# The last half of the final norm, in two pieces of 160 tokens, with two of eight tiles on GpSimd

## The chip, the core and the metric

The kernel runs on one core of a Trainium2 chip. The metric is device time in microseconds (us): the median of several runs, 925.3 us for the kernel before (three runs, 924.67 to 925.98). Beside the timed runs there is one profiled execution, from which every view below is taken; times inside it are counted from the start of its span.

## The reference, cut to what matters

The program computes one layer of a hybrid attention backbone for 128 prompt tokens and 512 latent tokens (640 in all, 1024 features), with an MLP of 4096 hidden features, and then a final RMS norm. Only the end concerns us:

```
x = x + gate2 * SquaredReLU-MLP(RMSNorm(x) * (1 + scale2) + shift2)
y = x * rsqrt(mean(x * x) + 1e-6) * final_norm_g
```

The mean runs over the 1024 features of one token.

## The kernel before

Activations lie with features on the partitions: 1024 features are eight tiles `X1[0]` to `X1[7]` of 128 partitions, each with 640 token columns in two halves of 320 (`HALVES`, also `L0` and `L1`). Float32 accuracy is had by splitting operands in a high and a low part, so that each product is three matmuls (L1657 to L1659).

The MLP is four chunks `c` of hidden features, each done as seven block products per pair of output tiles (`A11`, `A12`, `S3`, `A22`, `S2`, `S1`, `S4`) in the order of the list `SEQ`. A product is 12 matmuls into one PSUM bank. `layer2` then folds the bank into the residual: `gate_half` multiplies by the gate and adds to `X1` (VectorE, L1510). In the last chunk each finished half tile goes to `done_half`: ScalarE squares it (L1525), VectorE adds the squares up (L1529), ScalarE multiplies the tile by the norm's gain (L1530). For the second half of the tokens the tiles are finished in the order 1, 3, 5, 7 (`S1`), 0, 2, 4, 6 (`S4`); the last two squares are not added but summed by a matmul of their own (`NSUM[1] = 2`, list `direct[1]`). So the very last product of the program is `S4` with `n = 3`, and it finishes tile 6 of the second half.

With the last tile of a half, `done_half` appends nine small steps to the list `side`. The first, `norm`, sums acc and direct squares over the partitions with a matrix of ones (float32 matmuls, L1537) into a bank, and makes the reciprocal root from it as Exp(-0.5 Ln(mean + eps)) on ScalarE (L1541, L1542), kept in the SBUF tile `rstd3`. The other eight, `final(0)` to `final(7)`, multiply one half tile by the root on VectorE (L1546) and store it (L1547): even tiles on the SP queue, odd tiles on ScalarE's queue, 160 KB each. The main loop takes one step of `side` after each product (L1684), and all that are left when the products are through (L1686). The first half's steps lie in the same list, five empty steps behind its last product (`LAG3`); in the program text its last six `final` steps stand behind the last `gate_half`.

That text is not the order on the engines. The order written by hand ends at L1616; after it the framework places each instruction by when it expects its inputs, and it may put a later one ahead of an earlier one that is not ready. It also sets all waits between engines.

Of the kernel before, what the change touches and what calls it, by code (L numbers as in the profile page):

```python
# [12 lines left out]
AF = mybir.ActivationFunctionType  # L13
OP = mybir.AluOpType
# [4 lines left out]
HT = 320  # L19
KT = 8  # L20
# [42 lines left out]
NSUM = (1, 2)  # L63
# [2 lines left out]
P3 = 8  # L66
GPV = 1
LOACC = (("in", 21, 22), ("in", 29, 30), ("in", 20, 24), ("in", 25, 26), ("in", 28, 34), ("br", 0, 8))
FINP = ()
HALVES = (slice(0, HT), slice(HT, NT))  # L70


# [1 line left out]
def trunk_layer(ctx: ExitStack, tc: tile.TileContext, xT, small_in, wmodA, wmodB, tabs, cacheK, cacheV, bias,  # L74
                w_in, w_br, w_out, w1, w2, yT, akT, avT, bkT, bvT):
    nc = tc.nc
    PE, ACT, DVE = nc.tensor, nc.scalar, nc.vector
# [29 lines left out]
    def u(name, dt=F32):  # L107
        return cur["p"].tile([P, NT], dt, tag="u", bufs=cur["nu"], name=name)
# [10 lines left out]
    def tt_tile(name):  # L119
        return cur["p"].tile([P, NT], F32R, tag="tt", bufs=12, name=name)  # L120
# [22 lines left out]
    def r32(ap):  # L143
        return ap.bitcast(F32)
# [11 lines left out]
    gn = pk[:, 322:346].rearrange("p (k n) -> p k n", k=3)  # L156
    ones = cst.tile([P, P], F32, name="ones")
    DVE.memset(ones, 1.0 / 1024.0)
    eps = cst.tile([P, 1], F32, name="eps")
# [38 lines left out]
    def sq_add(acc, x, f, sl):  # L198

        q = acc if f == 0 else u("sq")  # L200
        ACT.activation(q[:, sl], x[:, sl], AF.Square)
        if 0 < f < KT - 1:
            DVE.tensor_add(acc[:, sl], acc[:, sl], q[:, sl])
        return q
# [933 lines left out]
    class Units:  # L1138
        n = 0
# [17 lines left out]
    for n in range(KT):  # L1157
# [4 lines left out]
        for i, w in enumerate((wa, wb)):  # L1162
            for h in range(2):
                if w is None:
                    s = u("sg")
# [68 lines left out]
    X1 = {}  # L1234
# [3 lines left out]
    for n, h in order(KT, 4):  # L1238
# [8 lines left out]
        sq = sq_add(acc2, X1[n], n, HALVES[h])  # L1247
# [31 lines left out]
    L0, L1 = slice(0, HT), slice(HT, NT)  # L1279
# [143 lines left out]
    def bank():  # L1423
        return pp8[0].tile([P, 512], F32, tag="b", bufs=8, name="b")[:, :HT]
# [22 lines left out]
    def opd(c, name):  # L1447
        if (c, name) not in OPD:
            OPD[c, name] = (bp[0].tile([P, 8, HT], F32R, tag="op3", bufs=1, name="op") if len(OPD) % 3 == 2 else
                            m.tile([P, 8, HT], F32R, tag="op", bufs=2, name="op"))  # L1450
        return OPD[c, name]
# [53 lines left out]
    def gate_half(i, src, h, g=None):  # L1505
        g = (mods if g is None else g)[:, 24 + i]

        off = HALVES[h].start
        for sl, j in SEGS[h]:
            DVE.scalar_tensor_tensor(X1[i][:, sl], src[:, sl.start - off:sl.stop - off], g[:, j:j + 1],  # L1510
                                     X1[i][:, sl], op0=OP.mult, op1=OP.add)

    nrm = {0: [], 1: []}
    direct = {0: [], 1: []}

    def done_half(i, h):

        x, first_, last_ = X1[i][:, HALVES[h]], not nrm[h], len(nrm[h]) == KT - 1
        if first_:
            nrm[h].append(tt_tile("acc3"))  # L1520
        else:
            nrm[h].append(None)
        acc = r32(nrm[h][0][:, L0])
        q = acc if first_ else r32(tt_tile("sq3")[:, L0])
        ACT.activation(q, x, AF.Square)  # L1525
        if len(nrm[h]) > KT - NSUM[h]:
            direct[h].append(q)
        elif not first_:
            (nc.gpsimd if SQP else DVE).tensor_add(acc, acc, q)  # L1529
        ACT.activation(x, x, AF.Copy, scale=gn[:, 2, i:i + 1])  # L1530
        if last_:
            rs = r32(tt_tile("rstd3")[:, L0])

            def norm():
                b = bank()
                for k, a in enumerate([acc] + direct[h]):
                    PE.matmul(b, ones, a, start=k == 0, stop=k == NSUM[h])  # L1537
                if POW:
                    DVE.tensor_scalar(rs, b, EPS, -0.5, op0=OP.add, op1=OP.pow)
                else:  # L1540
                    ACT.activation(rs, b, AF.Ln, bias=eps)  # L1541
                    ACT.activation(rs, rs, AF.Exp, scale=-0.5)  # L1542

            def final(f):
                y = X1[f][:, HALVES[h]]
                (DVE if h or f not in FINP else nc.gpsimd).tensor_mul(y, y, rs)  # L1546
                (nc.sync, nc.scalar)[f % 2].dma_start(yT[:, f, HALVES[h]], y)  # L1547
            side.extend([lambda: None] * (0 if h else LAG3) + [norm] + [lambda f=f: final(f) for f in range(KT)])

    WS = [None] * 4  # L1550

# [5 lines left out]
    def layer2(c, n, o, b, p):  # L1557
        if c < 3:
            if o == "A11":
                WS[n] = tp1.get()  # L1560
                ACT.activation(WS[n], b, AF.Copy)  # L1561
                gate_half(2 * n, WS[n] if GPV else b, 1)
            elif o == "S3":
                DVE.tensor_add(WS[n], WS[n], b)
            else:
                e, h = {"A12": (0, 0), "A22": (1, 0), "S2": (1, 0), "S1": (1, 1), "S4": (0, 1)}[o]
                gate_half(2 * n + e, b, h, neg if o == "S4" else None)
            return
        if o == "A11":
            p.pv = tp1.get()  # L1570
            ACT.activation(p.pv, b, AF.Copy)
            gate_half(2 * n, b, 1)
        if o == "A12":
            gate_half(2 * n, b, 0)
            done_half(2 * n, 0)
        if o == "S3":
            DVE.tensor_add(p.pv, p.pv, b)
        if o == "A22":
            p.x = tp2.get()
            DVE.tensor_sub(p.x, b, p.pv)  # L1580
            gate_half(2 * n + 1, p.pv, 1, neg)
        if o == "S2":
            DVE.tensor_add(p.x, p.x, b)
            gate_half(2 * n + 1, p.x, 0)
            done_half(2 * n + 1, 0)
        if o == "S1":
            gate_half(2 * n + 1, b, 1)
            done_half(2 * n + 1, 1)
        if o == "S4":
            gate_half(2 * n, b, 1, neg)  # L1590
            done_half(2 * n, 1)

# [5 lines left out]
    neg = parts[:, 1]  # L1598
# [15 lines left out]
    for n, h in todo:  # L1614
# [7 lines left out]
        e, i = n % 2, n // 2  # L1622
# [20 lines left out]
    for x in SEQ:  # L1643
        l, c, n, o = x
# [3 lines left out]
        else:  # L1648
            s = opd(c, XOF[o])
# [3 lines left out]
        b = getattr(p, "b" + whole) if whole else bank()  # L1653
        setattr(p, "b" + o, b)
        for k in range(4):
            xh, xl = xk(k)
            PE.matmul(b, w[:, k], xh, start=not whole and k == 0, stop=False, skip_group_check=True)  # L1657
            PE.matmul(b, w[:, k], xl, start=False, stop=False, skip_group_check=True)  # L1658
            PE.matmul(b, w[:, 4 + k], xh, start=False, stop=o not in ("A11", "S2", "S1") and k == 3, skip_group_check=True)  # L1659
        (layer1 if l == 1 else layer2)(c, n, o, b, p)  # L1660
        W.live -= 1
        if l == 1 and o in ("A12", "S2") and n > 1:
# [127 lines left out]
```

## Time and profile before

| quantity | value |
| --- | --- |
| median of three runs | 925.3 us |
| time of the profiled execution | 923.14 us |
| its span, first to last instruction | 921.4 us |
| granted TensorE clock, mean | 0.997 |
| TensorE matmul busy | 903.8 us, 98% |
| VectorE busy | 712.9 us, 77% |
| ScalarE busy | 564.4 us, 61% |
| GpSimd busy | 194.6 us, 21% |

The profiled execution has 1.7 us outside its span, and lies 2.2 us under the median of the timed runs. A busy share says little about the last 10 us, in which TensorE has run out of work: there the chain of waits and the timeline have to be read instruction by instruction.

### The profile page before, as it was taken

The numbers are of one execution on the slowest core, as the hardware profiler recorded it, in microseconds if no ns is written. First come the engines' busy times: TensorE is split into PE (matmuls) and PEld (weight loads), VectorE is DVE, ScalarE is ACT, GpSimd is POOL, SyncE is SP. The second block draws the span as 40 slices with busy tenths as digits, with TensorE's granted clock in tenths as the row PEclk, the third lists the DMA queues.
The fourth block names the chain that finished last, engine by engine and source line by source line (L and its number), as shares of the span: only waits on it lengthen the run. The fifth ranks groups of instructions, "written<-read, shape, count | busy, mean of one in ns | idle before, by whom it ended". The sixth has DMA issues, their size and how long they took to land.

```text
span 921.4 us, 16641 instructions
## 1 busy us (share of the span) xinstructions
PE 903.8 (98%) x6136; PEld 872.6 (95%) x6136; DVE 712.9 (77%) x1503; ACT 564.4 (61%) x1175; POOL 194.6 (21%) x225
## 2 busy tenths in 40 slices
PE   8999999999999999999999999999999999999996
PEld 6799889989999999999999999999999999999995
DVE  6675887857766697586689996986798778975897
ACT  4566777757656765755324577536754576447775
POOL 0020200002211001211130010445234432364140
PEclk9999999999999999999999999999999999999998
DMA  9893310115636389899742362888678877888475
GB/s 344 307 247 97 89 46 26 62 57 153 163 109 149 115 242 308 208 248 261 247 144 92 104 194 92 138 193 190 168 138 188 179 173 158 167 179 189 96 123 152
DMA packets 54321, 150.56 MB, mean 163 GB/s; under 512 B 6688, under 2 KB 10416, under 8 KB 54240
## 3 DMA queue, kind: packets, MB, share of 16 engines
q1 hardware_dynamic: 31440, 99.74, 32.9%
q0 software_dynamic: 21648, 48.45, 29.8%
q10 hardware_dynamic: 1152, 1.31, 0.4%
q8 instruction: 48, 0.79, 0.3%
q14 instruction: 33, 0.27, 0.1%
HBM read 137.15 MB, written 4.60 MB: 154 GB/s over the span
## 4 chain that ended last, share of the span: by engine, by line
PE 83%; DVE 7%; ACT 4%; DMA 3%; issue 2%; POOL 0%; DVEq 0%; SPq 0%; ACTq 0%; POOLq 0%
PE b L1657 12%; PE b L1658 12%; PE b L1659 12%; PE pg L315 6%; PE pg L316 6%; PE pg L317 6%; PE pss L317 3%; PE pss L315 3%; PE pss L316 3%; DVE mt L1102 2%; DMA wmt<-wmodB 2%; PE pt L317 2%; PE pt L315 2%; PE pt L316 2%; PE pt L694 1%
## 5 line engine op out<-in xcount | busy, mean ns | idle before, releaser
L1394 ACT ACTIVATE wb<-wsb 128x512 fp32r<-128x512 f32 x140 | 87.2, 628 | 89.5 <-PE b L1659 61.0
L1657 PE MATMUL b<-op,wb 128*128 128x320 f32 x448 | 138.6, 309 | 0.2 <-DVE x L1510 0.2
L1658 PE MATMUL b<-op,wb 128*128 128x320 f32 x448 | 138.5, 309 | 0.0
L1659 PE MATMUL b<-op,wb 128*128 128x320 f32 x448 | 138.4, 309 | 0.0
L1399 DVE TENSOR_TENSOR wb<-wsb,wb 128x512 fp32r<-128x512 f32 x124 | 91.5, 742 | 26.4 <-ACT wb L1394 26.3
L1402 POOL DMA_DIRECT2D wsb<-w x84 | 73.6, 911 | 128.6 <-DVE wb L1399 102.7
L1102 DVE SCALAR_TENSOR_TENSOR mt<-wmt,cb 128x512 f32<-128x512 f32 x128 | 80.7, 687 | 6.2 <-DMA wmt<-wmodB 6.2
L267 ACT ACTIVATE wh<-wst 128x512 fp32r<-128x512 f32 (+1 forms) x84 | 61.0, 740 | 39.7 <-PE pg L316 15.0
L1657 PEld LDWEIGHTS b<-op,wb 128*128 128x128 f32 x448 | 84.1, 188 | 0.9 <-DVE x L1510 0.9
L1658 PEld LDWEIGHTS b<-op,wb 128*128 128x128 f32 x448 | 84.1, 188 | 0.2 <-DVE op L1467 0.2
L1659 PEld LDWEIGHTS b<-op,wb 128*128 128x128 f32 x448 | 84.1, 188 | 0.0
L1379 POOL DMA_DIRECT2D wsb<-w x28 | 25.6, 914 | 137.2 <-DVE wb L1399 48.0
L633 DVE TENSOR_TENSOR pl<-pt,ph 128x512 fp32r<-128x512 f32 (+1 forms) x72 | 44.9, 627 | 12.0 <-ACT ph L632 10.1
L276 DVE TENSOR_TENSOR wl<-wst,wh 128x512 fp32r<-128x512 f32 (+1 forms) x55 | 43.0, 793 | 10.8 <-ACT wh L267 8.8
L1510 DVE SCALAR_TENSOR_TENSOR x<-b,parts,x 128x128 f32<-128x128 f32 (+1 forms) x116 | 46.3, 429 | 2.8 <-PE b L1659 2.0
L632 ACT ACTIVATE ph<-pt 128x512 fp32r<-128x512 f32 (+1 forms) x72 | 39.2, 548 | 13.9 <-PE po L702 3.9
L1394 ACT ACTIVATE wb<-wst 128x512 fp32r<-128x512 f32 x56 | 34.8, 626 | 16.2 <-PE b L1659 8.9
L1659 PE MATMUL b<-t,wb 128*128 128x320 f32 x144 | 44.5, 309 | 0.0
L1658 PE MATMUL b<-t,wb 128*128 128x320 f32 x144 | 44.5, 309 | 0.0
L1657 PE MATMUL b<-t,wb 128*128 128x320 f32 x144 | 44.5, 309 | 0.0
L1467 DVE TENSOR_TENSOR op<-hid,op 128x1280 fp32r<-128x1280 f32 (+2 forms) x32 | 36.9, 1155 | 7.6 <-ACT op L1466 7.4
L1510 DVE SCALAR_TENSOR_TENSOR x<-tp,parts,x 128x320 f32<-128x320 f32 (+2 forms) x60 | 38.5, 670 | 1.0 <-ACT tp L1561 1.0
(886 smaller groups left out, 3006.7 us busy)
## 6 DMA issues: line engine op xcount, KB each, us to landing
wsb<-w POOLq DMA_DIRECT2D x112, 256.0 KB, 5.2
wst<-w SPq DMA_DIRECT2D x36, 512.0 KB, 4.0
wmt<-wmodB SPq DMA_DIRECT2D x32, 512.0 KB, 4.4
wst<-w_in SPq DMA_DIRECT2D x31, 512.0 KB, 4.4
wsb<-w SPq DMA_DIRECT2D x28, 512.0 KB, 4.3
ms<-wmodA SPq DMA_DIRECT2D x16, 512.0 KB, 7.7
wl<-w_in POOLq DMA_DIRECT2D x9, 512.0 KB, 8.4
wst<-w_br SPq DMA_DIRECT2D x8, 512.0 KB, 6.5
```

Source lines behind the costliest of these rows:

```text
L267: ACT.activation(hi[:, ks], st[:, ks], AF.Copy)
L315: PE.matmul(ps, wh[:, k], xh[:, sl], start=first, stop=False)
L316: PE.matmul(ps, wh[:, k], xl[:, sl], start=False, stop=False)
L317: PE.matmul(ps, wl[:, k], xh[:, sl], start=False, stop=last)
L1102: DVE.scalar_tensor_tensor(t, st[:, q * 512:(q + 1) * 512], 1.0, r32(cb[2 * q + i][:, :512]), op0=OP.mult, op1=OP.mult, accum_out=parts[:, ...
L1394: ACT.activation(w[:, 0:4], t, AF.Copy)
L1399: (nc.gpsimd if o in BLKPOOL[l - 1] else DVE).tensor_sub(w[:, 4:8], t, r32(w[:, 0:4]))
L1402: nc.gpsimd.dma_start(t, self.src(l, c, n, e)[:, 4 * half:4 * half + 4], accum_op=OP.add)
L1510: DVE.scalar_tensor_tensor(X1[i][:, sl], src[:, sl.start - off:sl.stop - off], g[:, j:j + 1], X1[i][:, sl], op0=OP.mult, op1=OP.add)
L1657: PE.matmul(b, w[:, k], xh, start=not whole and k == 0, stop=False, skip_group_check=True)
L1658: PE.matmul(b, w[:, k], xl, start=False, stop=False, skip_group_check=True)
L1659: PE.matmul(b, w[:, 4 + k], xh, start=False, stop=o not in ("A11", "S2", "S1") and k == 3, skip_group_check=True)
```

## The change

The last product of the program (`S4`, `n = 3`) no longer goes through `gate_half`, `done_half` and `side`. It calls a new function, `last_half`, which does the end for the second half of the tokens:

- the gated sum of tile 6, its square and the three summing matmuls are done for columns 0 to 159 and then for 160 to 319, into one bank `s`;
- Ln writes to the SBUF tile `rs`, the first Exp writes back into the bank `s`, piece by piece; another Exp over all 320 columns makes the same root in SBUF, in `rs`;
- GpSimd multiplies tiles 0 and 1 by the root in SBUF; VectorE multiplies tiles 2, 3 and 4 piece by piece by the root in the bank, then 5, 7 and 6 whole. Tile 6 is not multiplied by its gain before (there is no L1530 for it); its last step multiplies by gain and root in one;
- each tile is stored whole, when both pieces are done, on the queue it had.

The first half of the tokens is untouched but for a choice of engine that was never used.

```
+FINP = (0, 1)
+FINQ = (2, 3, 4)
+FINW = (5, 7, 6)
+QUARTERS = (slice(0, HT // 2), slice(HT // 2, HT))
...
-                (DVE if h or f not in FINP else nc.gpsimd).tensor_mul(y, y, rs)
+                DVE.tensor_mul(y, y, rs)
...
+    def last_half(b):
+
+        i, g, sq = 6, neg[:, 30], r32(tt_tile("sq3")[:, L0])
+        rs, y = r32(tt_tile("rstd3")[:, L0]), [X1[f][:, L1] for f in range(KT)]
+        s = bank()
+        for q in QUARTERS:
+            DVE.scalar_tensor_tensor(y[i][:, q], b[:, q], g[:, 1:2], y[i][:, q], op0=OP.mult, op1=OP.add)
+            ACT.activation(sq[:, q], y[i][:, q], AF.Square)
+            for k, a in enumerate([r32(nrm[1][0][:, L0])] + direct[1] + [sq]):
+                PE.matmul(s[:, q], ones, a[:, q], start=k == 0, stop=k == NSUM[1])
+        for q in QUARTERS:
+            ACT.activation(rs[:, q], s[:, q], AF.Ln, bias=eps)
+            ACT.activation(s[:, q], rs[:, q], AF.Exp, scale=-0.5)
+        ACT.activation(rs, rs, AF.Exp, scale=-0.5)
+
+        def store(f):
+            (nc.sync, nc.scalar)[f % 2].dma_start(yT[:, f, L1], y[f])
+
+        for f in FINP:
+            nc.gpsimd.tensor_mul(y[f], y[f], rs)
+            store(f)
+        for q in QUARTERS:
+            for f in FINQ:
+                DVE.tensor_mul(y[f][:, q], y[f][:, q], s[:, q])
+                if q is QUARTERS[1]:
+                    store(f)
+        for f in FINW:
+            if f == i:
+                DVE.scalar_tensor_tensor(y[i], y[i], gn[:, 2, i:i + 1], s, op0=OP.mult, op1=OP.mult)
+            else:
+                DVE.tensor_mul(y[f], y[f], s)
+            store(f)
...
-        if o == "S4":
+        if o == "S4" and n == 3:
+            last_half(b)
+        elif o == "S4":
             gate_half(2 * n, b, 1, neg)
             done_half(2 * n, 1)
```

More of the change, by code (lines that the diff above doesn't have):

```diff
@@ L68 @@
 LOACC = (("in", 21, 22), ("in", 29, 30), ("in", 20, 24), ("in", 25, 26), ("in", 28, 34), ("br", 0, 8))
-FINP = ()
+FINP = (0, 1)
+FINQ = (2, 3, 4)
+FINW = (5, 7, 6)
+QUARTERS = (slice(0, HT // 2), slice(HT // 2, HT))
 HALVES = (slice(0, HT), slice(HT, NT))
```

## The prediction

> **What bounds the kernel now.** I read the page first: TensorE is busy nearly all of the span, so a change behind its last matmul can touch only the tail. Then the chain of waits from 912 us on, times from the span's start, lengths, instructions:
>
> ```profile
> span 921.4 us, 16641 instructions
> ```
>
> ```profile
> 911.76 0.47 DVE x L1510
> ...
> 912.25 0.48 ACT sq L1525
> ...
> 912.78 0.82 PE b L1537 x2
> ...
> 913.62 0.53 ACT rstd L1541
> ...
> 914.24 0.48 ACT rstd L1542
> ...
> 914.74 0.49 DVE x L1546
> ...
> 915.64 2.41 DVE x L1546 x6
> ```
>
> The tail is one thread: gated sum of tile 6, square, sum over partitions, Ln, Exp, then eight products at 0.40 each. By this view VectorE's products end the kernel at 918.05. But another 3.35 us follow, so I asked for the DMA in stretches of the tail (the last two columns are the share of the DMA engines and GB/s):
>
> ```profile
> 913.00:914.00 1.00, 0.58 (x2) 0.07 (x1) 0.82 (x3) 0.70 (x2) 0.00 (x0) 1.00 0.80 278
> 914.00:915.00 1.00, 0.00 (x0) 0.00 (x0) 0.26 (x1) 0.62 (x2) 0.00 (x0) 1.00 1.02 357
> 915.00:915.40 0.40, 0.00 (x0) 0.00 (x0) 0.40 (x2) 0.00 (x0) 0.00 (x0) 1.00 0.86 304
> 915.40:916.10 0.70, 0.00 (x0) 0.00 (x0) 0.70 (x3) 0.00 (x0) 0.00 (x0) 1.00 0.04 13
> 916.10:917.00 0.90, 0.00 (x0) 0.00 (x0) 0.90 (x3) 0.00 (x0) 0.00 (x0) 0.70 0.99 346
> 917.00:918.00 1.00, 0.00 (x0) 0.00 (x0) 1.00 (x3) 0.00 (x0) 0.00 (x0) 0.50 1.03 355
> 918.00:919.00 1.00, 0.00 (x0) 0.00 (x0) 0.05 (x1) 0.00 (x0) 0.00 (x0) 0.50 1.03 355
> 919.00:919.80 0.80, 0.00 (x0) 0.00 (x0) 0.00 (x0) 0.00 (x0) 0.00 (x0) 0.50 1.00 351
> 919.80:921.40 1.60, 0.00 (x0) 0.00 (x0) 0.00 (x0) 0.00 (x0) 0.00 (x0) 0.50 0.01 4
> ```
>
> ```profile
> yT<-x SPq DMA_DIRECT2D x8, 160.0 KB, 2.0
> yT<-x ACTq DMA_DIRECT2D x8, 160.0 KB, 2.0
> ```
>
> This is the view that decides. From 916.1 to 919.8 the DMA engines are full (share 0.99 to 1.03), at about 355 GB/s; the four stretches add up to 1.30 MB, the eight stores of 160 KB. So one store takes 3.7 / 8 = 0.46 us, more than the 0.40 of a product: **the stores, not the products, set the end**. The first store's tile is ready at 915.23 (914.74 + 0.49), its data flow 0.9 us later. So the end is: first tile ready + 0.9 + 3.7 + 1.6 = 921.4. Making the last products earlier gains nothing while the stores queue; only the *first* finished tile counts. The first half's stores still flow until 915.4, and the gap until 916.1 is 0.7 us: with the first half's stores where they are, no version of this tail can gain more than about 0.7 us, or 1.0 us with the slack of 913 to 914 (0.80 busy, 0.2 us) added.
>
> A median of this kernel can tell some 0.2% from no change: 1.85 us.
>
> **The change, part by part.** Prices by width come from pairs of rows for one engine:
>
> ```profile
> L1510 DVE SCALAR_TENSOR_TENSOR x<-b,parts,x 128x320 f32<-128x320 f32 x36 | 19.4, 545 | 2.7 <-PE b L1659 2.0 <-ACT tp L1571 0.5
> L1510 DVE SCALAR_TENSOR_TENSOR x<-b,parts,x 128x128 f32<-128x128 f32 x40 | 13.8, 345 | 0.1
> L1394 ACT ACTIVATE wb<-wsb 128x512 fp32r<-128x512 f32 x140 | 87.2, 628 | 89.5 <-PE b L1659 61.0 <-DMA wsb<-w 21.9 <-DVE wb L1399 3.9
> L1525 ACT ACTIVATE sq<-x 128x320 f32<-128x320 f32 x14 | 6.3, 460 | 0.9 <-DVE x L1510 0.9
> ```
>
> VectorE: 200 ns for 192 columns, so a piece of 160 saves 0.17 of 0.545: 0.38 us. ScalarE: 168 ns for 192 columns, so a piece saves 0.14. Halving the width does not halve the time: each extra instruction has a floor.
>
> *Gated sum and square.* The VectorE queue around it:
>
> ```profile
> 910.47 1.28 DVE L1546 TENSOR_TENSOR x<-x,rstd 128x320 f32<-128x320 f32 x3
> 911.68 0.54 DVE L1510 SCALAR_TENSOR_TENSOR x<-b,parts,x 128x320 f32<-128x320 f32 x1
> 912.14 1.69 DVE L1546 TENSOR_TENSOR x<-x,rstd 128x320 f32<-128x320 f32 x4
> 914.74 3.31 DVE L1546 TENSOR_TENSOR x<-x,rstd 128x320 f32<-128x320 f32 x8 [0.92 <-ACT rstd L1542]
> ```
>
> Nothing ahead of the gated sum changes, so it starts at 911.68 again, behind three products of the first half. Its first piece ends at 912.06, its second at 912.36 (0.08 overlaps). The squares take 0.46 - 0.14 = 0.32 each: 912.08 to 912.40 and 912.38 to 912.70. So the first square is 0.3 us earlier than the whole one (912.73).
>
> *Summing.* Before, two of the three matmuls ran while the square was awaited:
>
> ```profile
> 902.90 0.70 PE L1537 MATMUL b<-acc,ones 128*128 128x320 f32 x2
> 903.44 0.70 PE L1537 MATMUL b<-sq,ones 128*128 128x320 f32 x2
> 903.99 0.41 PE L1657 MATMUL b<-op,wb 128*128 128x320 f32 x1
> ```
>
> Start to start such a sum of 320 columns takes 0.54, so 160 take 0.27 (estimate). In the order of the text, acc and the direct square of the second piece stand behind the first piece's square. So from 912.45 four of them follow each other; the last starts at 913.26 and needs 0.82 - 0.27 = 0.55 to its end: 913.81, against 913.60 before. If the framework puts those two ahead, the sum ends at 912.75 + 0.55 = 913.30. I take the order of the text, since all six write one bank. The Trainium skill ("PSUM — Partial Sum Buffer", section "The four PSUM rules") says that a second accumulation begun in a bank before the first is through spoils it, which speaks for that order; no run here shows it.
>
> *Ln and Exp.* Two pieces of 0.53 - 0.14 = 0.39 and two of 0.48 - 0.14 = 0.34 make 1.46, less some 0.1 where the engine overlaps them, against 1.10 before (913.62 to 914.72). Does the first piece run on without the second? They share the bank `s`. What the waits do with one bank and two engines is shown here:
>
> ```profile
> 863.28 0.42 ACT L1571 ACTIVATE tp<-b 128x320 f32<-128x320 f32 x1
> 863.73 0.55 DVE L1510 SCALAR_TENSOR_TENSOR x<-b,parts,x 128x320 f32<-128x320 f32 x1 [0.50 <-ACT tp L1571]
> ```
>
> L1571 copies the bank to an SBUF tile, and L1572 calls `gate_half` with the same bank, not with the copy. Both only read the bank, yet VectorE sat idle 0.50 us until ScalarE was through. So two engines are kept apart on one bank even where neither writes. I take it that this holds for different columns too. Then Ln of the first piece waits for the last matmul of the second (913.81), and VectorE's first product, on columns 0 to 159, waits for the Exp that writes columns 160 to 319: the root is usable from 913.83 + 1.46 - 0.1 = 915.2, against 914.72. The page named above states just that in its section "PSUM bank collisions raise a hardware error": two engines must be guarded by bank (and partition quadrant), not by address, reads against reads included; the row above agrees for equal columns, and by the page the sum is the one I make.
>
> *Products.* A product steps at (3.31 - 0.48) / 7 = 0.40, so a piece at 0.24, and lasts 0.32. Tile 2 is whole after the fourth piece: 915.22 + 3 x 0.24 + 0.32 = 916.26. Before, the first whole tile was ready at 915.23. Here the change pays twice: it works on three tiles at once, so none is done early. VectorE then ends near 918.0 with six tiles, as it did before with eight; all are ready before the DMA reaches them.
>
> *GpSimd.* The second Exp chain's copy in SBUF costs ScalarE another 0.48 behind 915.2, so GpSimd starts at 915.7. Its nearest rows:
>
> ```profile
> L1399 POOL TENSOR_TENSOR wb<-wsb,wb 128x512 fp32r<-128x512 f32 x12 | 16.5, 1373 | 6.1 <-ACT wb L1394 6.0
> L273 POOL TENSOR_TENSOR wl<-wst,wh 128x1024 fp32r<-128x1024 f32 x3 | 7.2, 2411 | 22.0 <-ACT wh L267 22.0
> L566 POOL TENSOR_TENSOR rt<-raw,cos 128x512 f32<-128x512 f32 x1 | 1.6, 1613 | 4.6 <-DVE raw L561 4.6
> ```
>
> ```profile
> 642.87 0.49 DVE L1494 TENSOR_TENSOR tp<-b,tp 128x320 f32<-128x320 f32 x1
> 642.92 1.30 POOL L1399 TENSOR_TENSOR wb<-wsb,wb 128x512 fp32r<-128x512 f32 x1 [0.94 <-ACT wb L1394]
> 643.64 0.49 DVE L1502 TENSOR_TENSOR tp<-tp,b 128x320 f32<-128x320 f32 x1 [0.28 <-PE b L1659]
> ```
>
> From 512 to 1024 columns it is 2.0 to 2.2 ns a column, so 320 columns cost 1.30 - 0.42 = 0.88 at best and 1.61 - 0.39 = 1.2 at worst. VectorE with one operand in a bank, as in all its new products, did not disturb GpSimd's 1.30, nor GpSimd its 0.49; I charge nothing for the two together. Tiles 0 and 1 are ready at 916.6 to 916.9 and 917.5 to 918.1. The DMA is busy with the other six until 916.26 + 0.9 + 6 x 0.46 = 919.9, so both cost nothing, as long as they do not stand first in their queues (below). The gain for GpSimd is equally nothing: VectorE was not what ended last.
>
> *L1530 for tile 6* goes: it ran beside the sum, so nothing is saved. The folded gain in the last product costs 0.06 there, behind the queue of stores: nothing.
>
> *Sum.* First tile ready at 916.26 instead of 915.23: +1.0 us. With the two matmuls moved ahead, +0.5 us. I take +0.9, near the first, since its reason (one bank, one order) is the same that holds Ln back. Span 922.3, profiled execution 924.0 (from 923.14), median 925.3 + 0.9 = **926.2 us**: 0.1%, within what can be told from no change. The median lies 2.2 us over the profiled execution; I carry the difference over.
>
> **The rivals.** *The pieces do overlap* (the waits go by columns, not by bank). Ln starts on the first sum at 912.45 + 0.55 = 913.0, Exp ends at 913.75; the second sum ends at 913.81, its Exp at 914.56. VectorE does the first three pieces in between, and tile 2 is whole at 914.58 + 0.32 = 914.9: 0.35 us earlier than before, so 924.95 us. For it: no row shows two engines on different columns of one bank. Against it: the wait at 863.73, between two mere readers.
>
> *GpSimd's stores head their queues.* Stores of tiles 0 and 1 stand first in the text on SP's and ScalarE's queue; an issue that waits for GpSimd holds back 2, 4, 6 and 3, 5, 7. Data then flow from 916.6 to 916.9 + 0.9 = 917.5 to 917.8, and the eight stores end 3.7 later: +1.4 to +1.7, 926.7 to 927.0. Against it: the framework places an issue by when it expects the tile.
>
> *First-half products fall behind* (slower). `last_half` now stands in the text ahead of the first half's leftover `final` steps, four of which ran at 912.14. If VectorE takes its new work first, their stores come last, 0.46 each: four make 1.8 on top of 1.0, +2.8, 928.1 us. With two behind (+1.9) the 0.2% is passed. Against it: VectorE is idle from 912.4 to 915.2, room for all four (1.69), and at 910.47 three of them ran ahead of a gated sum that stands ahead of two of them in the text.
>
> *The products set the end after all* (faster): with the pieces overlapping, GpSimd's second tile is ready at 915.05 + 2 x 0.88 = 916.8 instead of 918.05: -1.25, 924.05 us, still under 0.2%. Against it: the full DMA engines from 916.1 on.
>
> **How the numbers follow.** Bank held: 0.58; pieces overlap: 0.16; queue heads: 0.10; first half behind: 0.11; products set the end: 0.05. The first three lie within 0.2%, and so does most of the last; for scatter of medians (0.65 either way above) and for what I do not see I give faster 0.06 and slower 0.13, same 0.81. Range: from the overlapping pieces (924.95) less the scatter, 924.3, to the queue heads (927.0) and a little over, 927.2.
>
> **What would show it.** In the changed profile: ScalarE's first Ln starts only behind the sixth sum; VectorE's first product starts behind the second Exp on the bank, near 915.2; no store's data flow between 915.4 and about 917; then about 355 GB/s for 3.7 us and 1.6 us of end. Wrong it is, if VectorE's first products start near 913.8, if L1546 stands behind the new products, or if the DMA engines pause between the last eight stores.

## The result and the profile after

The median went from 925.31 us (22 runs) to 927.86 us (22 runs): ratio 1.0026, 95% interval 1.0016 to 1.0036, so about 2.4 us slower, between 1.5 and 3.3. The interval leaves out 1, so the slowdown is small but real. 927.86 us lies 0.66 above the upper end of the predicted range.

The profiled execution took 928.31 us (before: 923.14), its span is this:

```profile
span 926.2 us, 16660 instructions
```

Not all of the 4.8 us between the two spans belongs to the change. On every engine the same instructions stand in the same order up to the last gated sum (but for the summing matmuls just ahead of it, which the change cuts in two), yet that sum starts at 911.68 us before and at 914.77 after. Such a shift needs no change of the program: two profiles of one unchanged experiment kernel, below, differ there by 1.1 us, and a kernel that differs from the kernel before only in its last stores (half the bytes, below) has this sum at 916.15. So I count the **tail**: from the start of the last gated sum to the end of the span. It is 921.4 - 911.68 = 9.72 us before and 926.2 - 914.77 = 11.43 after: +1.71, inside the interval of the ratio. (Spans are given to 0.1, so a tail is good to 0.05, and a difference of two tails to 0.1.)

A second part lies outside the span. A run's time less its span was 1.73 to 1.84 us in the 29 runs of the kernel before that were taken beside the experiments in rounds, 1.79 on average. It was 2.06 to 2.15 in the 22 runs of the changed kernel, 2.11 on average: +0.3 us. Every experiment kernel below that calls `last_half` has 2.06 to 2.18, and the one that doesn't has 1.76. What in `last_half` costs this, no run shows.

The timeline of the tail after; columns are start, length, engine, line, operation, output and inputs, and in brackets the idle time before and what ended it:

```profile
914.77 0.68 DVE L1559 SCALAR_TENSOR_TENSOR x<-b,parts,x 128x160 f32<-128x160 f32 x2
...
917.05 0.39 ACT L1564 ACTIVATE rstd<-b,eps 128x160 f32<-128x160 f32 x1 [1.14 <-DVE x L1549]
...
917.48 0.31 ACT L1565 ACTIVATE b<-rstd 128x160 f32<-128x160 f32 x1
917.82 0.39 ACT L1564 ACTIVATE rstd<-b,eps 128x160 f32<-128x160 f32 x1
918.25 0.31 ACT L1565 ACTIVATE b<-rstd 128x160 f32<-128x160 f32 x1
918.59 0.47 ACT L1566 ACTIVATE rstd<-rstd 128x320 f32<-128x320 f32 x1
918.59 1.48 DVE L1576 TENSOR_TENSOR x<-x,b 128x160 f32<-128x160 f32 x6 [1.54 <-ACT b L1565]
919.14 1.68 POOL L1572 TENSOR_TENSOR x<-x,rstd 128x320 f32<-128x320 f32 x2 [13.71 <-ACT rstd L1566]
...
920.02 1.81 SPq L1569 DMA_DIRECT2D yT<-x  x4
...
920.85 2.31 ACTq L1569 DMA_DIRECT2D yT<-x  x4
```

Read it against the prediction's rows. Two Ln and two Exp follow each other without an overlap, 917.05 to 918.56. VectorE's first product starts at 918.59, 3.82 after the gated sum; before it was 914.74 - 911.68 = 3.06. Tile 2 is whole after the fourth of the six products: 918.59 + 3 x 0.23 + 0.32 = 919.60, 4.83 after the gated sum against 3.55. Yet the first store is issued at 920.02 and ScalarE's queue issues its first at 920.85. These two times are the ends of GpSimd's products: 919.14 + 0.86 = 920.00 and 919.14 + 1.68 = 920.82. The waits of SP's queue name it (in total, times, longest, us):

```profile
SPq L1569 <- POOL x L1572: 2.9, 1, 2.9
```

The DMA in stretches of the tail after (busy time of the five engines with counts, clock, DMA share, GB/s):

```profile
918.50:919.00 0.50, 0.00 (x0) 0.00 (x0) 0.41 (x2) 0.47 (x2) 0.00 (x0) 1.00 0.17 59
919.00:920.00 1.00, 0.00 (x0) 0.00 (x0) 1.00 (x6) 0.06 (x1) 0.86 (x2) 0.89 0.00 0
920.00:920.50 0.50, 0.00 (x0) 0.00 (x0) 0.50 (x3) 0.00 (x0) 0.50 (x1) 0.50 0.00 0
920.50:921.00 0.50, 0.00 (x0) 0.00 (x0) 0.50 (x2) 0.00 (x0) 0.32 (x1) 0.50 0.25 87
921.00:922.00 1.00, 0.00 (x0) 0.00 (x0) 0.32 (x1) 0.00 (x0) 0.00 (x0) 0.50 1.00 347
922.00:923.00 1.00, 0.00 (x0) 0.00 (x0) 0.00 (x0) 0.00 (x0) 0.00 (x0) 0.50 1.02 355
923.00:924.00 1.00, 0.00 (x0) 0.00 (x0) 0.00 (x0) 0.00 (x0) 0.00 (x0) 0.50 1.02 356
924.00:924.60 0.60, 0.00 (x0) 0.00 (x0) 0.00 (x0) 0.00 (x0) 0.00 (x0) 0.50 0.97 341
924.60:926.20 1.60, 0.00 (x0) 0.00 (x0) 0.00 (x0) 0.00 (x0) 0.00 (x0) 0.50 0.01 3
```

Nothing moves from 919.0 to 920.5. The half microsecond after that carries 87 of 355 GB/s, a quarter of it, so data start near 920.88. Then the engines are full for 3.7 us, and 1.6 us of end follow, as before. The whole loss of the tail is in the time until the first store's data, which splits by these rows into the root +0.76 (3.82 against 3.06), the first whole tile behind it +0.52 (1.01 against 0.49), and from that tile to data +0.4 (920.88 - 919.60 = 1.28 against 0.87): 1.7 in all.

### The profile page after: what moved, and what is told of

It is laid out like the page before. It is cut to its first block, busy times and chain, and to the rows that moved or that the text cites. A ratio compares the mean times of both kernels' runs of the same rounds, so it can differ in the third digit from the quotient of the medians.

```text
span 926.2 us, 16660 instructions
## 1 busy us (share of the span) xinstructions
PE 904.9 (98%) x6142; PEld 873.3 (94%) x6142; DVE 712.2 (77%) x1505; ACT 564.6 (61%) x1178; POOL 196.7 (21%) x227
## 3 DMA queue, kind: packets, MB, share of 16 engines
q10 hardware_dynamic: 1152, 1.31, 0.4%
## 4 chain that ended last, share of the span: by engine, by line
PE 79%; DVE 7%; DMA 5%; ACT 4%; issue 3%; POOL 1%; SPq 0%; DVEq 0%; POOLq 0%; ACTq 0%
PE b L1696 11%; PE b L1695 11%; PE b L1697 11%; PE pg L318 6%; PE pg L319 6%; PE pg L320 6%; PE pss L320 3%; PE pss L318 3%; PE pss L319 3%; PE pt L320 2%; PE pt L319 2%; PE pt L318 2%; DVE mt L1105 2%; PE pt L697 1%; PE pss L410 1%
```

## The experiments

**My theory** after reading this: two parts of the change cost in the tail, and nothing else does. Both pieces lie in one bank, so the engines work on them one after another, three tiles at a time (1.25 us). And GpSimd's two tiles stand first in both store queues, though the tiles behind them are whole earlier: tile 0 at 5.23 after the gated sum ahead of tile 2 at 4.83, tile 1 at 6.05 ahead of tile 3 at 5.06 (0.45 us). **The rivals**: the products themselves have got too slow and set the end; or something else in the program became slower, since the ratio's 2.4 us is above the tail's 1.7. The profiled executions of these kernels lie between 923.6 and 928.4 us and the kernel before moves as much (923.8 and 927.9 beside them), so the tails are compared; each is from one profile. In the edits, `...` marks where lines are left out.

**GpSimd's stores in a queue of their own**, to take the heads away and leave all else:

```
-            (nc.sync, nc.scalar)[f % 2].dma_start(yT[:, f, L1], y[f])
+            (nc.sync if f in FINP else nc.scalar).dma_start(yT[:, f, L1], y[f])
```

> The changed kernel, with the stores of GpSimd's tiles 0 and 1 alone on SP's queue and the six others on ScalarE's, so that no store waits behind one of GpSimd's. Measured in the profile from the start of the first gated-sum piece to the end of the span: 9.72 us before, 11.43 in the changed kernel. Theory (two terms): the queues cost 0.4, the longer chain to the first whole tile 1.3; so 11.0 us, with the first store issued when tile 2 is whole, 4.85 after the gated sum. Rival (the queues are the whole of it): 9.7 to 9.9. Rival (GpSimd's queue order costs nothing, since the DMA engines catch up): 11.4.

Its span is 921.5 us; its timeline shows:

```profile
910.55 0.67 DVE L1559 SCALAR_TENSOR_TENSOR x<-b,parts,x 128x160 f32<-128x160 f32 x2
...
914.91 1.67 POOL L1572 TENSOR_TENSOR x<-x,rstd 128x320 f32<-128x320 f32 x2 [13.70 <-ACT rstd L1566]
915.40 3.15 ACTq L1569 DMA_DIRECT2D yT<-x  x6
...
915.80 1.15 SPq L1569 DMA_DIRECT2D yT<-x  x2
```

The first store (tile 2, ScalarE's queue) is issued 915.40 - 910.55 = 4.85 after the gated sum instead of 5.25, as soon as the tile is whole, and 0.4 us before GpSimd's first tile. The tail is 10.95: 0.48 less than after the change. The heads of the queues cost about that much, no more.

**The same, tile by tile**, to split the rest: both pieces of a tile one after the other.

```
-        for q in QUARTERS:
-            for f in FINQ:
+        for f in FINQ:
+            for q in QUARTERS:
...
```

> As queues_split (one bank, GpSimd's two stores alone on SP), but VectorE does both pieces of a tile one after the other, so that tile 2 is whole after the second product and not after the fourth. Theory (the tail follows the first whole tile, and three tiles at once cost two product steps of 0.23 us): first store about 4.4 us after the gated sum instead of 4.85, a tail of 10.5 us instead of 10.97; what then remains over the 9.72 of before is the longer chain to the root, 0.75. Rival (the bank's columns of piece 1 and piece 2 cost the first products something besides): the tail stays over 10.7.

The span is 923.1 us:

```profile
912.61 0.67 DVE L1559 SCALAR_TENSOR_TENSOR x<-b,parts,x 128x160 f32<-128x160 f32 x2
...
917.00 3.14 ACTq L1569 DMA_DIRECT2D yT<-x  x6
```

GpSimd's stores are on SP alone here too. First store at 4.39, tail 10.5, both as expected: working on three tiles at once cost some 0.5. What is left over 9.72 is 0.8, and the later root (0.76) accounts for it within the 0.1 that two tails can tell.

**A bank for each piece.** VectorE does the last three tiles by pieces here too:

```
-        s = bank()
+        S = {0: bank(), HT // 2: bank()}
         for q in QUARTERS:
+            s = S[q.start]
...
```

> The changed kernel with a bank of its own for each piece, so that Ln and Exp of the first piece, and VectorE's products on it, need not wait for the second. Theory (one bank is what holds the pieces together): the first Ln starts about 0.8 earlier, 1.5 after the gated sum; tile 2 is whole 3.6 after the gated sum instead of 4.83; 9.7 to 9.9 us from gated sum to end, as before the change. Rival (the waits between two engines go by columns, and the first products are late for another reason): nothing moves, 11.4.

The span is 925.2 us:

```profile
915.49 0.67 DVE L1560 SCALAR_TENSOR_TENSOR x<-b,parts,x 128x160 f32<-128x160 f32 x2
...
916.95 0.39 ACT L1566 ACTIVATE rstd<-b,eps 128x160 f32<-128x160 f32 x1 [0.32 <-PE b L1563]
...
917.72 0.78 DVE L1578 TENSOR_TENSOR x<-x,b 128x160 f32<-128x160 f32 x3
...
918.99 2.29 SPq L1571 DMA_DIRECT2D yT<-x  x4
919.07 1.68 POOL L1574 TENSOR_TENSOR x<-x,rstd 128x320 f32<-128x320 f32 x2 [12.92 <-ACT rstd L1568]
```

Now the pieces overlap: Ln of the first piece starts 1.46 after the gated sum (2.28 in one bank), VectorE's first product at 2.23 (3.82), between the two Exps. The first whole tile is stored at 3.50, and the tail is 9.7, the tail of before. Here the framework also put GpSimd's stores behind those of tiles 2 and 3. So with a second bank both losses are gone, and still nothing is gained: the first whole tile is hardly earlier than before (3.55).

Since 1.7 us of tail stood against 2.4 us of ratio, this kernel was timed in rounds too:

> The same kernel as in two_banks, timed in rounds. Theory (the whole loss lies in the tail: pieces in one bank and GpSimd's stores at the head of both queues): the tail from the first gated sum to the end of the span was 9.76 us in its profile against 9.72 before, so the time is that of the kernel before within 0.1%: ratio 0.999 to 1.001. Rival (something ahead of the tail is slower too, for instance code or tiles that have moved, which would be the 0.7 us by which the ratio of the changed kernel, +2.4 us, passes its tail's +1.7): ratio 1.001 or more.

Ratio 1.0011, interval 0.9995 to 1.0026 (926.01 us, 12 runs, against 925.39, 29 runs). This is no measurable change, and it decides nothing between the two: the value lies on the rival's side, the interval on both, and an excess of 0.7 us outside the tail (0.08%) lies inside it. What these 12 runs do show is the time outside the span: 2.12 us on average against 1.79, with a tail as before. The second profile of this same kernel has a tail of 9.7 again, with the gated sum at 916.59 where the first had 915.49: that much an execution drifted here by itself.

**One piece**, the change without its pieces: GpSimd, the root in the bank and the folded gain stay, and GpSimd's stores come last in the text.

```
-QUARTERS = (slice(0, HT // 2), slice(HT // 2, HT))
+QUARTERS = (slice(0, HT),)
...
```

> The changed kernel with all 320 columns as one piece; GpSimd still has tiles 0 and 1, and the root is kept in the bank. Theory (stores set the end, and the pieces were the cost): the first tile is whole 3.55 after the gated sum as before the change, VectorE is through 0.8 us earlier than before the change with six tiles, and the end is where it was: 9.7 to 9.9 us. Rival (products set the end): 0.8 less than before, 8.9. Rival (GpSimd or the third Exp is the cost): 11 or more.

The span is 922.3 us:

```profile
912.50 0.55 DVE L1559 SCALAR_TENSOR_TENSOR x<-b,parts,x 128x320 f32<-128x320 f32 x1
...
914.44 0.53 ACT L1564 ACTIVATE rstd<-b,eps 128x320 f32<-128x320 f32 x1 [0.90 <-PE b L1562]
...
915.54 1.28 DVE L1575 TENSOR_TENSOR x<-x,b 128x320 f32<-128x320 f32 x3 [0.89 <-ACT b L1565]
916.06 2.38 SPq L1569 DMA_DIRECT2D yT<-x  x4
...
917.54 0.54 DVE L1580 SCALAR_TENSOR_TENSOR x<-x,pk,b 128x320 f32<-128x320 f32 x1
```

VectorE is through 5.58 after the gated sum, where before it needed 6.37 (914.74 + 3.31 - 911.68), yet the tail is 9.8. So 0.8 us less of products on VectorE are worth nothing: the rival that the products set the end is refuted, and with it the worth of giving tiles to GpSimd. The Ln here is marked as waiting for PE, the sum. In the changed kernel the same Ln is put down to VectorE's L1549, which ended there within 0.03 us of the sum, and the view names the later of the two. Ln doesn't need those four products: with two banks it started at 916.95, while they ran from 916.07 to 917.76.

**Half the bytes**: the kernel before, storing only columns 0 to 159 of each tile of the second half. The other half of that result is left out.

```
-                (nc.sync, nc.scalar)[f % 2].dma_start(yT[:, f, HALVES[h]], y)
+                n = HT // 2 if h else HT
+                (nc.sync, nc.scalar)[f % 2].dma_start(yT[:, f, HALVES[h].start:HALVES[h].start + n], y[:, :n])
```

> The kernel before, but each store of the second half writes only the first 160 of its 320 columns (half of the second half's result is left out). Everything up to the stores is unchanged. If the stores set the end by their bytes, eight of them take 1.85 instead of 3.7 us, and the end follows the last product instead: 9.1 us from gated sum to end, against 9.72. If a store's price goes by rows and not by bytes, or the products set the end anyway: 9.6 to 9.7.

The span is 925.3 us, the gated sum starts at 916.15, the tail is 9.1. Its products, and its DMA behind the first tile:

```profile
919.22 3.31 DVE L1546 TENSOR_TENSOR x<-x,rstd 128x320 f32<-128x320 f32 x8 [0.92 <-ACT rstd L1542]
```

```profile
920.60:921.50 0.90, 0.00 (x0) 0.00 (x0) 0.90 (x3) 0.00 (x0) 0.00 (x0) 1.00 0.71 206
921.50:922.50 1.00, 0.00 (x0) 0.00 (x0) 1.00 (x3) 0.00 (x0) 0.00 (x0) 0.86 0.75 213
```

With 80 KB a store the rate falls to 206 GB/s: one store per product, 81,920 bytes / 0.40 us = 205. Now the products set the pace, and the tail is 0.6 shorter though they are unchanged. With 160 KB the stores did.

**The root in SBUF, piece by piece**, to see whether the bank holds the engines apart. Ln still reads the one bank; Exp writes to SBUF, and all products read it there. GpSimd's stores are alone on SP, as in the first experiment.

```
-            ACT.activation(s[:, q], rs[:, q], AF.Exp, scale=-0.5)
-        ACT.activation(rs, rs, AF.Exp, scale=-0.5)
+            ACT.activation(rs[:, q], rs[:, q], AF.Exp, scale=-0.5)
...
-                DVE.tensor_mul(y[f][:, q], y[f][:, q], s[:, q])
+                DVE.tensor_mul(y[f][:, q], y[f][:, q], rs[:, q])
...
```

> As queues_split, but the root goes to SBUF piece by piece and all products read it there; the third Exp is gone, the sum is still in one bank. Theory (it is the bank that keeps the engines apart, not the order of the text): ScalarE's first Ln still waits for the sixth sum, 2.28 us after the gated sum, but VectorE's first product starts right behind the first Exp, at about 3.05 instead of 3.81, tile 2 is whole at about 4.15, and the tail is 10.2 to 10.4 us instead of 10.97. Rival (VectorE waits for both pieces for a reason other than the bank): first product at about 3.8 as in queues_split, tail near 10.9. Side question: GpSimd's products now run beside VectorE products with both operands in SBUF; if those disturb each other, GpSimd's 0.85 us or VectorE's 0.31 us get longer.

The span is 923.9 us. First its timeline, then how long its piece products took (shortest, median, longest, in ns), then the groups of the changed kernel for the same work, and last its DMA:

```profile
912.90 0.67 DVE L1559 SCALAR_TENSOR_TENSOR x<-b,parts,x 128x160 f32<-128x160 f32 x2
...
915.18 0.68 ACT L1564 ACTIVATE rstd<-b,eps 128x160 f32<-128x160 f32 x2 [1.14 <-DVE x L1549]
915.75 0.33 ACT L1565 ACTIVATE rstd<-rstd 128x160 f32<-128x160 f32 x1
...
915.97 0.33 ACT L1565 ACTIVATE rstd<-rstd 128x160 f32<-128x160 f32 x1
...
916.11 2.83 DVE L1575 TENSOR_TENSOR x<-x,rstd 128x160 f32<-128x160 f32 x6 [0.94 <-ACT rstd L1565]
916.39 1.00 POOL L1571 TENSOR_TENSOR x<-x,rstd 128x320 f32<-128x320 f32 x1 [12.83 <-ACT rstd L1565]
...
917.36 0.93 POOL L1571 TENSOR_TENSOR x<-x,rstd 128x320 f32<-128x320 f32 x1
```

```profile
L1575 DVE TENSOR_TENSOR x<-x,rstd x6: 310/322/981, 916.1 to 918.6; 128x160 f32<-128x160 f32 x6
```

```profile
L1572 POOL TENSOR_TENSOR x<-x,rstd 128x320 f32<-128x320 f32 x2 | 1.7, 856 | 13.7 <-ACT rstd L1566 13.7
L1576 DVE TENSOR_TENSOR x<-x,b 128x160 f32<-128x160 f32 x6 | 1.5, 316 | 1.5 <-ACT b L1565 1.5
```

```profile
917.40:918.00 0.60, 0.00 (x0) 0.00 (x0) 0.60 (x2) 0.00 (x0) 0.60 (x1) 1.00 0.00 0
918.00:919.50 1.50, 0.00 (x0) 0.00 (x0) 1.50 (x5) 0.00 (x0) 0.29 (x1) 0.60 0.53 189
```

The first Ln still waits 2.28 for the sixth sum, and VectorE's first product starts 3.21 after the gated sum, 0.03 behind the first Exp on SBUF (915.75 + 0.33). Without the bank VectorE doesn't wait for the second piece: this part of the theory held. The tail didn't: 11.0 instead of 10.2 to 10.4. The side question gives the reason. With both operands in SBUF, VectorE's products beside GpSimd take up to 0.98 instead of 0.31, and GpSimd's 0.93 to 1.00 instead of 0.86; six products need 2.83 us instead of 1.48. The first store goes out earlier than in the first experiment (GpSimd's first tile at 917.42, 4.52 after the gated sum, against 4.85), but the six on ScalarE's queue start only at 918.50, and until 919.5 the DMA engines are half busy. So the first store alone doesn't decide: those behind it must keep the engines full. The Trainium skill ("SBUF — State Buffer", section "Who interferes with whom") states that a VectorE instruction with two SBUF inputs contends with a GpSimd one that reads SBUF, and that with at most one SBUF input (outside two-port modes) it doesn't; the two pairs of numbers agree with both halves. So with GpSimd beside VectorE a root in SBUF, though ready 0.6 us earlier (3.21 against 3.82), made the tail no shorter than the root in the bank (11.0 against 10.95).

**Could the first store come earlier?** If the time of the first store counts most, the way to gain is to store pieces. With two banks, tiles 2 and 3 go out in pieces, the first ones on SP ahead of GpSimd's tiles:

```
+        for q in QUARTERS:
+            for f in FINE:
+                mul(f, q)
+                store(nc.scalar if q.start else nc.sync, f, q)
...
```

> Two banks, and tiles 2 and 3 stored piece by piece, the first pieces ahead of GpSimd's tiles. Theory (the first finished part sets the end, then the stores run without a pause): the first piece is ready about 2.55 us after the gated sum instead of 3.55, its data flow from about 3.4 to 3.5, before the first half's last store ends near 3.95, and the eight stores follow without a gap: a tail of 9.2 to 9.4 us against 9.72 before, 0.05% of the time, which rounds can hardly tell from no change. Rival (rows of 640 bytes instead of 1280 cost the DMA engines more, and the four piece stores lose what the earlier start brings): four stores of 80 KB take 0.3 us or more each instead of 0.23, and the tail is 9.6 us or more.

The gated sum starts at 914.99, the span is 924.5 us:

```profile
917.57 3.04 SPq L1571 DMA_DIRECT2D yT<-x  x4
```

```profile
917.80:918.40 0.60, 0.00 (x0) 0.00 (x0) 0.60 (x4) 0.57 (x2) 0.00 (x0) 1.00 1.04 359
918.40:919.50 1.10, 0.00 (x0) 0.00 (x0) 1.10 (x6) 0.09 (x1) 0.92 (x2) 0.97 0.98 303
919.50:920.50 1.00, 0.00 (x0) 0.00 (x0) 0.71 (x3) 0.00 (x0) 0.75 (x1) 0.50 0.65 208
920.50:922.90 2.40, 0.00 (x0) 0.00 (x0) 0.00 (x0) 0.00 (x0) 0.00 (x0) 0.50 1.03 356
```

The first piece goes out 2.58 after the gated sum, and the gap behind the first half's stores is filled. But from 918.4 the rate falls to 303 and then 208 GB/s. In the second of these stretches the engines are 0.65 busy: pieces of 80 KB were issued 0.4 to 0.5 us apart, too little to keep them full. In the first they are 0.98 busy and still move less. So shorter rows have a price of their own. The run with half the bytes, where all eight stores have rows of 640 bytes, gives it: 206 GB/s at a share of 0.71 would be 290 at a full share, where rows of 1280 bytes moved 355 at 1.02. By this estimate a store of 80 KB takes 0.28 us, between the theory's 0.23 and the rival's 0.3 or more. The tail is 9.5, 0.2 less than before, about half of what I expected, and shorter than the rival had it; the ratio is 0.9998 (0.9980 to 1.0017).

Last, the gains of the norm folded into VectorE's products, and four tiles in pieces:

```
-                DVE.tensor_mul(y, y, rs)
+                DVE.scalar_tensor_tensor(y, y, gn[:, 2, f:f + 1], rs, op0=OP.mult, op1=OP.mult)
...
```

> As early_pieces, and the gains of the last norm are folded into VectorE's last products (ScalarE no longer scales those tiles), with four tiles stored piece by piece. Theory: ScalarE is free earlier in the first half too, so the first half's stores end earlier, and nothing but the eight stores of the second half stands behind the first piece: a tail of 8.8 to 9.2 us, 0.06 to 0.1% of the time. Rival (the first half's stores wait for VectorE's products, not for ScalarE's scaling): the same tail as early_pieces, or longer, since two more tiles are stored in pieces and the products with a folded gain last 0.54 instead of 0.48.

```profile
912.57 1.93 DVE L1550 SCALAR_TENSOR_TENSOR x<-x,pk,rstd 128x320 f32<-128x320 f32 x4
...
914.57 0.36 ACTq L1551 DMA_DIRECT2D yT<-x  x1
```

```profile
913.00:914.70 1.70, 0.61 (x5) 0.37 (x3) 1.70 (x5) 1.33 (x6) 0.00 (x0) 1.00 0.44 154
```

The tail is 10.3 (span 922.3, gated sum at 911.98); the theory fell. The first half's last four products take 1.93 us instead of 1.69 and end at 914.50, 2.52 after the gated sum (before 912.14 + 1.69 - 911.68 = 2.15); the last store follows at 914.57. The DMA is 0.44 busy in that stretch, and these stores are done in the time of the second half: from 914.70 to 920.64 the engines moved 1.81 MB, 0.5 more than the second half's 1.31. (The gated sum itself starts 0.35 behind the start of the last product's last matmul here and 0.69 before and in the other kernels, so of the 0.6 us some 0.3 is real loss.) The ratio is 1.0007 (0.9990 to 1.0023). No version here beats the kernel before by what can be measured; each that was timed in rounds also carries the 0.3 us outside the span.

## Why the prediction was wrong

**What held.** The stores set the end (one piece, half the bytes). The end is first data + 3.7 + 1.6. One bank kept the pieces apart: first Ln behind the sixth sum, VectorE's first product behind the second Exp. With two banks both went away. The Trainium skill ("PSUM — Partial Sum Buffer", section "PSUM bank collisions raise a hardware error") has the rule to guard by bank and quadrant, not by address; the two runs agree with it for different columns of one bank. The first half's products kept their place. GpSimd's 0.86 is the low bound, 0.88, and VectorE did not disturb it.

**What failed.** The main step: of GpSimd's tiles, "both cost nothing, as long as they do not stand first in their queues". They stood first, on both queues, so the 0.9 us from the first whole tile to data became 1.28, a term of 0.4 us that the sum had at nothing. The rival of the queue heads had just this mechanism at +1.4 to +1.7, 926.7 to 927.0 us; the tail gave +1.71. That the size fits as well is partly luck: its upper end came from 1.2 us for a GpSimd product, which took 0.86, while GpSimd started 0.35 us later than forecast (919.14 - 914.77 + 911.68 = 916.05 for 915.7). I gave this rival 0.10, on the word that the framework places an issue by when it expects the tile. It doesn't go by the text alone: with two banks it put the stores of tiles 2 and 3 ahead of GpSimd's, which stand first in the text. But here it issued tile 0 ahead of tile 2, which was whole 0.40 us earlier, and tile 1 ahead of tile 3, 1.0 us earlier. No run shows how it comes to its expectation.

**What was sized too small.** The chain to the root. I took 1.46 less 0.1 of overlap for two Ln and two Exp; they took 1.51 from 917.05 to 918.56, with no overlap. No row of before had shown one: Ln and Exp at 913.62 and 914.24 don't overlap either. The same four in the order Ln, Ln, Exp, Exp overlapped in the kernel with the root in SBUF: 1.12 from 915.18 to the end of the second Exp. The sum over partitions ended 2.25 after the gated sum, where I had 2.13. And of the +1.0 that these steps gave I took +0.9; the first whole tile came +1.28 later.

**What was left out.** I carried the median over from the span, as if the time outside it stayed the same. It grew by 0.3 us, in every kernel with `last_half`.

**How far this goes.** The tail's 1.7 and the 0.3 outside the span make 2.0 of the ratio's 2.4 us, or 927.3 us, just past the range. The tail alone would have given 927.0, inside it. The rest is 0.4 us of the ratio; its interval reaches down to 1.5, so nothing more need be there, and that nothing is was not shown.

The rival of overlapping pieces was too hopeful as well: with two banks the pieces did overlap, but the first store went out less than 0.1 us earlier against the gated sum, where this rival had 0.35.

## What to carry to other kernels

When the DMA engines are full in the tail, ask when the first finished store is issued, and whether those behind it keep the engines full: splitting a step pays there if the first *whole* output comes earlier. Two pieces that shared one PSUM bank didn't overlap here from the sum on; give each its own bank. Look at each store queue's head: the store of a tile that a helper engine finishes late must not stand ahead of tiles that are whole. If GpSimd multiplies beside VectorE, try to let VectorE read one operand from PSUM. And compare the time outside the span too: it can change with the program.

## What the runs showed of the hardware that was not expected

- VectorE products of 128x160 floats with both operands in SBUF took 0.98 us beside a GpSimd product (0.32 at the median, with those that ran clear of it), and 0.31 beside it with one operand in PSUM.
- Ln, Exp, Ln, Exp of 160 columns on ScalarE, through one bank, took 1.51 us; Ln, Ln, Exp, Exp with the root in SBUF took 1.12.
- Stores of 80 KB (rows of 640 bytes), issued 0.40 us apart, moved 206 GB/s at a DMA share of 0.71, or 290 at a full share by estimate; stores of 160 KB (rows of 1280 bytes) at the same pace moved 355 at a share of 1.03.
- The time of a run outside its span was 1.79 us for the kernel before and 2.11 for the changed one, with no overlap between the runs.
